# The last x tile of a stage before weight splits on VectorE, and modulation units spread over later stages

## The chip, the cores and the metric

One NeuronCore of one Trainium2 chip runs the whole program. The metric is the device time of one execution in microseconds (us); the time before is the median of three runs. TensorE is PE below (its weight loads PEld), VectorE is DVE, ScalarE ACT, GpSimd POOL, and SyncE (SP) issues most of the transfers.

## What is computed

Two blocks on x of 256 tokens by 1024. The first has a Mamba-2 mixer, a convolutional feed-forward, a differential attention and a second feed-forward; the second block, whose scale, shift and gate come from a vector c, has a sparse attention with a top-k (`dsa` in the kernel) beside a gated recurrence, and a third feed-forward. Every stage starts with an RMS norm and ends by adding to x. Cut to what the change touches:

```python
# first block, per layer:   x = x + mixer(rms_norm(x) * g);  x = x + conv_ffn(rms_norm(x) * g)
# second block:
c_act = silu(c)
mod = c_act @ w_ada + b_ada                       # w_ada is 1024 x 6144
sh1, sc1, ga1, sh2, sc2, ga2 = split(mod, 6)
xn = rms_norm(h, g_mix) * (1.0 + sc1) + sh1
q, k, v, qi, ki, wi, xr, yr, gate_a, gate_b = split(xn @ w_in + b_in)
attn = dsa_attention(q, k, v, qi, ki, wi, rel_bias)
rnn = rg_lru(causal_dwconv(xr)) * gelu(yr)
h = h + ga1 * ((sigmoid(gate_a) * (attn @ w_o_attn) + sigmoid(gate_b) * (rnn @ w_o_rnn)) @ w_out)
xn = rms_norm(h, g_ffn) * (1.0 + sc2) + sh2
val, gte = split(causal_dwconv(xn @ w_up))
h = h + ga2 * ((silu(gte) * val) @ w_down)
return rms_norm(h, g_final)
```

So `sh1` and `sc1` are needed where the sparse stage starts, `ga1` at its last product, `sh2` and `sc2` at the start of the last feed-forward and `ga2` at its last product.

## The kernel before

x lies transposed in SBUF as eight tiles of 128 features by 256 tokens. The stages run one after the other: mamba, ffn0, attn, ffn1, dsa, ffn2. Every weight product is made in fp32 from hi and lo parts: per 128 rows of a weight three matmuls of 128x128 by 256 columns, hi by hi, hi by lo and lo by hi (`mmB`, L381 to L383; in attention's token form L925 to L927). A *piece* is a weight tile of up to 128 by 1024 and serves 24 matmuls; one output tile of an up projection is one piece and one *step*.

A piece comes in a raw chunk (`load_chunk`, L230, on SP, four buffers), and is *split* (`split`, L242): ACT copies `wh` (L253), DVE subtracts for `wl` (L257; POOL does so for nine pieces). `step()` (L303) runs after each product: it calls posts that are due, splits up to two pieces ahead (as many as `LEADS` says, at most five), and issues modulation units.

**Starts of stages.** When an output tile m of a stage's last product is done, `add_x` (L508) adds it to x on DVE (L511, L513 with the gate), squares it (ACT L442, running sum on POOL L446), and `mkraw` (L395) makes hi (ACT L398) and lo (DVE L399) of the unnormalised tile, times its gain. The next stage's first four output tiles (`tileR`) use these, so that they need no norm, and are scaled afterwards. The norm itself: `rstd_bc` (L448) sums the squares with two matmuls over `sqacc` and two over the last tile's `sq` (L454), DVE (L296) and POOL (L297, a power) make the reciprocal root, PE broadcasts it (L465), ACT copies it (`rsb`, L486), then DVE makes `ny` (L495) and the lo parts `xl` (L471, or L500 with a shift). Attention needs the root per token only and has no broadcast; its first product is `tok("k", 0)` (L913), two halves of tokens with 24 matmuls each.

**Modulation.** `mod` is made by 96 *units*: one loads 256 KB of `w_ada` (L556, SP) into one of two buffers and multiplies it with silu(c) on DVE, summing along the row (L558); per two units a sum of 128 by 1 follows (`mod`, L562). `ADA_UNITS` gives for a part of a stage the steps from a to b in which n units are issued; each is ordered behind the last split on DVE (`self.pace`).

**Order.** The engines' orders are fixed when the program is built: a scheduler places the instructions by the order of the code, the dependencies and its estimate of when each can run; `after` adds a dependence that only orders.

The sparse stage's end, to which the prediction comes: eight tiles of yr (posts L1302: a gelu on ACT, `yg` on DVE L1306), then hi and lo of the eight `yg` tiles (`split_act`, L469; ACT L470, DVE L471), then per output tile m a product with `w_o_attn` and one with `w_o_rnn`, then `w_out`.

## Time and profile before

| | us |
|---|---|
| median of three runs | 1171.66 (1169.17 to 1174.88) |
| profiled execution | 1170.62 |
| its span | 1168.8, mean granted clock 0.979 |
| PE busy | 1119.3 (96%) |
| DVE busy | 949.9 (81%) |
| ACT busy | 711.2 (61%) |
| POOL busy | 171.7 (15%) |

The span runs from the first to the last instruction of the profiled execution; the rest of its time lies around it. [...] In a timeline each row has its start, its duration, engine, source line, operation, result and operands, and in brackets how long the engine had been idle before it and what ended that.

### The profile page before, as it was taken

The numbers are of one execution on the slowest core, as the hardware profiler recorded it, in microseconds if no ns is written. First come the engines' busy times: TensorE is split into PE (matmuls) and PEld (weight loads), VectorE is DVE, ScalarE is ACT, GpSimd is POOL, SyncE is SP. The second block draws the span as 40 slices with busy tenths as digits, with TensorE's granted clock in tenths as the row PEclk, the third lists the DMA queues.
The fourth block names the chain that finished last, engine by engine and source line by source line (L and its number), as shares of the span: only waits on it lengthen the run. The fifth ranks groups of instructions, "written<-read, shape, count | busy, mean of one in ns | idle before, by whom it ended". The sixth has DMA issues, their size and how long they took to land. (4 is left out here: it accounts for less than half of the span.)

```text
span 1168.8 us, 23504 instructions
## 1 busy us (share of the span) xinstructions
PE 1119.3 (96%) x9174; PEld 1090.0 (93%) x9174; DVE 949.9 (81%) x1884; ACT 711.2 (61%) x1322; POOL 171.7 (15%) x162
## 2 busy tenths in 40 slices
PE   6899998999999989999999999899999999999997
PEld 5799887999999989888899999899999999999997
DVE  5987998788899878787899988768877888888742
ACT  6567555576666546877666664465587657666541
POOL 3202665201100103222000001100100020000010
PEclk8899989999999989999999999999999999999999
DMA  8355442548766886654376667844542653554530
GB/s 307 137 181 191 161 157 79 191 170 275 262 204 238 283 288 231 199 188 153 123 248 207 213 225 257 298 175 151 180 165 94 215 214 125 203 181 176 180 132 36
DMA packets 50190, 224.80 MB, mean 192 GB/s; under 512 B 5744, under 2 KB 10496, under 8 KB 31136
## 3 DMA queue, kind: packets, MB, share of 16 engines
q1 hardware_dynamic: 41616, 211.53, 52.3%
q10 hardware_dynamic: 7056, 7.46, 2.1%
q0 software_dynamic: 1408, 4.32, 1.1%
q8 instruction: 72, 1.18, 0.4%
q14 instruction: 38, 0.31, 0.1%
HBM read 222.11 MB, written 4.25 MB: 194 GB/s over the span
## 5 line engine op out<-in xcount | busy, mean ns | idle before, releaser
L253 ACT ACTIVATE wh<-raw 128x1024 fp32r<-128x1024 f32 (+2 forms) x360 | 369.9, 1031 | 275.6 <-PE mm L382 237.9
L257 DVE TENSOR_TENSOR wl<-raw,wh 128x1024 fp32r<-128x1024 f32 (+1 forms) x351 | 419.7, 1197 | 107.4 <-ACT wh L253 105.1
L381 PE MATMUL mm<-xh,wh 128*128 128x256 f32 x1624 | 464.1, 286 | 3.0 <-DVE cv L632 1.7
L382 PE MATMUL mm<-xl,wh 128*128 128x256 f32 x1624 | 459.9, 283 | 4.1 <-DVE xl L471 3.8
L383 PE MATMUL mm<-xh,wl 128*128 128x256 f32 x1624 | 459.6, 283 | 0.1
L381 PEld LDWEIGHTS mm<-xh,wh 128*128 128x128 f32 x1624 | 307.7, 190 | 7.9 <-issue 3.5
L382 PEld LDWEIGHTS mm<-xl,wh 128*128 128x128 f32 x1624 | 307.7, 190 | 5.5 <-DVE xl L471 4.7
L383 PEld LDWEIGHTS mm<-xh,wl 128*128 128x128 f32 x1624 | 307.5, 189 | 0.6 <-DVE xc L1225 0.3
L381 PE MATMUL mm<-hh,wh 128*128 128x256 f32 x528 | 147.4, 279 | 0.0
L383 PE MATMUL mm<-hh,wl 128*128 128x256 f32 x528 | 147.4, 279 | 0.0
L382 PE MATMUL mm<-hl,wh 128*128 128x256 f32 x528 | 147.4, 279 | 0.0
L446 POOL TENSOR_TENSOR sqacc<-sqacc,sq 128x256 f32<-128x256 f32 x42 | 50.0, 1192 | 629.4 <-issue 365.2
L823 DVE SCALAR_TENSOR_TENSOR cv<-mm,par,cv 128x255 f32<-128x255 f32 x240 | 114.7, 479 | 1.8 <-ACT cv L821 0.2
L381 PEld LDWEIGHTS mm<-hh,wh 128*128 128x128 f32 x528 | 99.2, 188 | 0.0
L382 PEld LDWEIGHTS mm<-hl,wh 128*128 128x128 f32 x528 | 99.2, 188 | 0.0
L383 PEld LDWEIGHTS mm<-hh,wl 128*128 128x128 f32 x528 | 99.2, 188 | 0.0
L558 DVE SCALAR_TENSOR_TENSOR ada<-ada,silu_c 128x512 f32<-128x512 f32 x96 | 66.3, 701 | 20.8 <-DMA ada<-in_wada_dram 20.3
L821 ACT ACTIVATE cv<-mm,par 128x256 f32<-128x256 f32 x120 | 65.7, 547 | 0.3 <-PE mm L383 0.3
L381 PE MATMUL mm<-rw,wh 128*128 128x256 f32 (+2 forms) x168 | 51.8, 309 | 9.4 <-ACT wh L253 8.6
L442 ACT ACTIVATE sq<-x 128x256 f32<-128x256 f32 x49 | 20.0, 410 | 57.8 <-DVE x L511 43.7
L382 PE MATMUL mm<-rw,wh 128*128 128x256 f32 (+2 forms) x168 | 51.7, 308 | 0.0
L383 PE MATMUL mm<-rw,wl 128*128 128x256 f32 (+2 forms) x168 | 51.1, 305 | 0.0
(305 smaller groups left out, 1900.6 us busy)
## 6 DMA issues: line engine op xcount, KB each, us to landing
raw<-in_w_dram SPq DMA_DIRECT2D x148, 1024.0 KB, 4.9
ada<-in_wada_dram SPq DMA_DIRECT2D x96, 256.0 KB, 4.2
raw<-in_w_dram SPq DMA_DIRECT2D x23, 896.0 KB, 4.6
raw<-in_w_dram SPq DMA_DIRECT2D x6, 768.0 KB, 4.3
abc<-acs_scr ACTq DMA_DIRECT2D x16, 256.0 KB, 3.3
rel_bias_scr<-rel_bias_row POOLq DMA_DIRECT2D x8, 384.0 KB, 6.7
bias<-rel_bias_scr ACTq DMA_DIRECT2D x16, 128.0 KB, 2.6
x<-in_xT_dram SPq DMA_DIRECT2D x4, 256.0 KB, 4.2
```

What stands on the lines that cost most here:

```text
L253: nc.scalar.activation(wh[:, :n], src, AF.Copy)
L257: self.pace = nc.vector.tensor_tensor(wl[:, :n], src, wh[:, :n].bitcast(F32), op=ALU.subtract)
L381: nc.tensor.matmul(out, h, xh[:, k, :], start=first and a == 0, stop=False)
L382: nc.tensor.matmul(out, h, xl[:, k, :], start=False, stop=False)
L383: nc.tensor.matmul(out, l, xh[:, k, :], start=False, stop=last and a == n - 1)
L442: nc.scalar.activation(s, self.x[:, k, :], AF.Square)
L446: nc.gpsimd.tensor_tensor(self.acc, self.acc, s, op=ALU.add)
L558: i = nc.vector.scalar_tensor_tensor(t, t, 1.0, self.sc[:, h * 512:h * 512 + 512], op0=ALU.mult, op1=ALU.mult, accum_out=self.part[:, h, m ...
L821: nc.scalar.activation(c, pt, AF.Identity, scale=w(2), bias=P(cb, ct))
L823: nc.vector.scalar_tensor_tensor(c[:, d:], pt[:, :T - d], w(2 - d), c[:, d:], op0=ALU.mult, op1=ALU.add)
```

## The change

1. **`gate`.** In `mkraw`, DVE's lo part of the last x tile (k = 7) is remembered, and splits issued after it, up to the end of the next step, are ordered behind it on DVE. While the last output tile of a stage is made (`out_tile(7)`), at most `END_LEAD` = 3 pieces are split ahead, until its `add_x`.
2. **Attention's norm.** `rstd_bc` is called inside the first `tok`, and its matmuls are ordered behind the 24 of the first half of tokens.
3. **`ADA_UNITS`.** Before: nine units per up projection of ffn0 and ffn1, up to 30 in each of their down projections, 16 in attention, six in its output. Now 14 in ffn0's down projection, 16 in attention, eight and 14 in ffn1, 28 in the sparse stage (steps 4 to 57), 16 in the up projection of ffn2 (steps 12 to 39), none in the rest. `ada_until` makes up what a stage needs, should it not be there.
4. **`ada_load`.** A unit's load is issued before the DVE instruction of the unit ahead of it, in place of right before its own.
5. Buffers of the sparse stage share names (`th`, `mt1` in `xru`; `mt2` in `at2`; `kid` in a second `vT`); the modulation's buffers stay open to the end of the program.

```diff
+END_LEAD = 3
 QK_LAG, O_LAG = 3, 3
 ADA_AT = 8
-ADA_UNITS = {"up": (20, 44, 9), "down": (1, 19, 30), "attn": (5, 22, 16), "attn_out": (1, 6, 6)}
+ADA_UNITS = {"ffn0": (20, 44, 0), "ffn0_out": (1, 16, 14), "attn": (5, 22, 16), "attn_out": (0, 1, 0), "ffn1": (20, 44, 8),
+             "ffn1_out": (1, 16, 14), "dsa": (4, 58, 28), "dsa_out": (0, 1, 0), "ffn2": (12, 40, 16),
+             "ffn2_out": (0, 1, 0)}
...
             self.pace = nc.vector.tensor_tensor(wl[:, :n], src, wh[:, :n].bitcast(F32), op=ALU.subtract)
+            if self.gate is not None:
+                self.after(self.pace, self.gate)
...
-        lead = lead[self.since - 1] if self.since <= len(lead) else self.NS
+        lead = min(lead[self.since - 1] if self.since <= len(lead) else self.NS, self.cap)
         for _ in range(2):
             if self.ns < self.nu + lead:
                 self.split(self.since in POOLED.get(self.part_of, ()))
+        self.gate = None
...
-            nc.vector.scalar_tensor_tensor(l[:, k, 0:T], self.x[:, k, :], g(k), h[:, k, 0:T].bitcast(F32),
-                                           op0=ALU.mult, op1=ALU.subtract)
+            i = nc.vector.scalar_tensor_tensor(l[:, k, 0:T], self.x[:, k, :], g(k), h[:, k, 0:T].bitcast(F32),
+                                               op0=ALU.mult, op1=ALU.subtract)
+            if k == 7 and self.now:
+                self.gate = i
...
-    def rstd_bc(self, parts, n, bcast=True):
+    def rstd_bc(self, parts, n, bcast=True, behind=None):
 
         nc = self.nc
         st = self.ax()
         for i, p in enumerate(parts):
             for tt in range(2):
-                nc.tensor.matmul(st[:, tt:tt + 1], p[:, tt * 128:tt * 128 + 128], self.ones,
+                mm = nc.tensor.matmul(st[:, tt:tt + 1], p[:, tt * 128:tt * 128 + 128], self.ones,
                                  start=(i == 0 and tt == 0), stop=i == len(parts) - 1, skip_group_check=True)
+                if behind is not None:
+                    self.after(mm, behind)
...
+        if m == 7:
+            self.cap = self.NS
+
+    def out_tile(self, m):
+
+        if m == 7:
+            self.cap = END_LEAD
...
+    def ada_load(self):
+        m, h = self.adal[self.adan]
+        self.adan += 1
+        t = self.adap.tile([128, D // 2], F32, name="ada")
+        w = self.a["wada"]
+        self.nc.sync.dma_start(t, bass.AP(tensor=w.tensor, offset=w.offset + (2 * m + h) * 65536,
+                                          ap=[[D // 2, 128], [1, D // 2]]))
+        self.adat.append(t)
...
+            while len(self.adat) < 2 and self.adan < len(self.adal):
+                self.ada_load()
             m, h = self.adaq.popleft()
-            t = self.adap.tile([128, D // 2], F32, name="ada")
-            nc.sync.dma_start(t, bass.AP(tensor=w.tensor, offset=w.offset + (2 * m + h) * 65536,
-                                         ap=[[D // 2, 128], [1, D // 2]]))
+            t = self.adat.popleft()
...
+    def ada_until(self, m):
+
+        n = 2 * m - (96 - len(self.adaq))
+        if n > 0:
+            self.due = 0.0
+            self.ada(n)
...
-        self.rstd_bc([self.acc, self.sq7], D, bcast=False)
-        rs = self.rs
         xop = {"k": (rkv[:, 0], rkv[:, 1]), "v": (rkv[:, 0], rkv[:, 1]), "q": rq}
         v = tl("v", [128, 2, 1024])
         tT = {}
+        norm = []
...
-                    nc.tensor.matmul(o, xl[:, k, s], wh[:, cs], start=False, stop=k == 7)
+                    mm = nc.tensor.matmul(o, xl[:, k, s], wh[:, cs], start=False, stop=k == 7)
+                if not norm:
+                    self.rstd_bc([self.acc, self.sq7], D, bcast=False, behind=mm)
+                    norm.append(self.rs)
...
+                    self.ada_until(16 if n == "dsa" else 40)
```

Where the instructions stand now. The first place is the start of attention on DVE, at the add of the last x tile (`x`, L511 before and L522 now; `rw` and `xl0` are lo parts of raw tiles, `ada` modulation units, `wl` splits). Before:

```order
L558 SCALAR_TENSOR_TENSOR ada_5031,mod_parts_3206<-ada_5031,silu_c_3207 128x512 [waits DMAHW3_49]
L558 SCALAR_TENSOR_TENSOR ada_5034,mod_parts_3206<-ada_5034,silu_c_3207 128x512 [waits DMAHW4_49]
L257 TENSOR_TENSOR wl_5328<-raw_5104,wh_5327 128x1024 [waits PE_49,Activation_49]
L562 SCALAR_TENSOR_TENSOR mod_3205<-mod_parts_3206,par_81 128x1 [waits DVE_49]
L511 TENSOR_TENSOR x_83<-mm_5272,x_83 128x256 [waits PE_49]
L897 TENSOR_TENSOR lam2_5367<-par_81 128x128
L257 TENSOR_TENSOR wl_5357<-raw_5104,wh_5356 128x1024 [waits Activation_49]
L399 SCALAR_TENSOR_TENSOR rw_4536<-x_83,par_81,rw_4536 128x256 [waits DVE_49,Activation_49]
L399 SCALAR_TENSOR_TENSOR xl0_4538<-x_83,par_81,xh0_4537 128x256 [waits Activation_49]
```

and with the change:

```order
L406 SCALAR_TENSOR_TENSOR rw_4505<-x_83,par_81,rw_4505 128x256 [waits DVE_49,Activation_49]
L406 SCALAR_TENSOR_TENSOR xl0_4507<-x_83,par_81,xh0_4506 128x256 [waits Activation_49]
L522 TENSOR_TENSOR x_83<-mm_5187,x_83 128x256 [waits PE_49]
L935 TENSOR_TENSOR lam2_5276<-par_81 128x128
L943 TENSOR_SCALAR sg_5283<-par_81 128x1
L937 TENSOR_REDUCE lam_5278<-lam2_5276 128x2 [waits DVE_49]
L406 SCALAR_TENSOR_TENSOR rw_4505<-x_83,par_81,rw_4505 128x256 [waits Activation_49]
L406 SCALAR_TENSOR_TENSOR xl0_4507<-x_83,par_81,xh0_4506 128x256 [waits Activation_49]
L261 TENSOR_TENSOR wl_5262<-raw_4968,wh_5261 128x1024
L261 TENSOR_TENSOR wl_5268<-raw_5036,wh_5267 128x1024 [waits DMAHW2_49]
```

Before, two units, a split and a `mod` sum stand ahead of the last add, and a split behind it ahead of its lo parts. With the change the add comes right behind the lo part of the tile before it, and the splits come behind its lo parts.

On PE at the same place, the sum over the last tile's squares (`sq`) stood inside the first token tile before:

```order
L926 MATMUL mm_5387<-wl_5269,rw_4536 128x256 [waits DVE_49]
L927 MATMUL mm_5387<-wh_5268,rw_4536 128x256
L925 MATMUL mm_5387<-wh_5268,rw_4536 128x256
L454 MATMUL ax_5376<-onec_86,sq_5350 128x1 [waits Activation_49]
L454 MATMUL ax_5376<-onec_86,sq_5350 128x1
L926 MATMUL mm_5387<-wl_5269,rw_4536 128x256
L927 MATMUL mm_5387<-wh_5268,rw_4536 128x256
```

and now stands, with the sum over `sqacc`, behind its last matmul (`rw` with `wh_5183` is the end of the first half; `wh_5151` begins the second):

```order
L962 MATMUL mm_5288<-wh_5183,rw_4505 128x256 [waits Activation_49]
L963 MATMUL mm_5288<-wl_5184,rw_4505 128x256
L964 MATMUL mm_5288<-wh_5183,rw_4505 128x256 [waits DVE_49]
L463 MATMUL ax_5313<-onec_86,sqacc_4591 128x1 [waits Pool_49]
L463 MATMUL ax_5313<-onec_86,sqacc_4591 128x1
L463 MATMUL ax_5313<-onec_86,sq_5255 128x1 x2
L962 MATMUL mm_5288<-wh_5151,rw_4505 128x256
L963 MATMUL mm_5288<-wl_5152,rw_4505 128x256
```

The second place is the start of the sparse stage on DVE (`gmdsa` is the gain with modulation, `rs` the root's first step). Before:

```order
L257 TENSOR_TENSOR wl_9464<-raw_9254,wh_9463 128x1024 [waits PE_49,Activation_49]
L511 TENSOR_TENSOR x_83<-mm_9408,x_83 128x256 [waits PE_49]
L257 TENSOR_TENSOR wl_9491<-raw_9254,wh_9490 128x1024 [waits Activation_49]
L399 SCALAR_TENSOR_TENSOR rw_8693<-x_83,gmdsa_8694,rw_8693 128x256 [waits DVE_49,Activation_49]
L558 SCALAR_TENSOR_TENSOR ada_9221,mod_parts_3206<-ada_9221,silu_c_3207 128x512 [waits DMAHW5_49]
L558 SCALAR_TENSOR_TENSOR ada_9256,mod_parts_3206<-ada_9256,silu_c_3207 128x512 [waits DMAHW6_49]
L562 SCALAR_TENSOR_TENSOR mod_3205<-mod_parts_3206,par_81 128x1 [waits DVE_49]
L296 TENSOR_SCALAR rs_9508<-ax_9503 128x2 [waits PE_49]
```

and with the change, where no unit is left and the last add comes behind a lo part:

```order
L522 TENSOR_TENSOR x_83<-mm_9169,x_83 128x256 [waits PE_49]
L261 TENSOR_TENSOR wl_9253<-raw_9043,wh_9252 128x1024 [waits DMAHW7_49,Activation_49]
L406 SCALAR_TENSOR_TENSOR rw_8587<-x_83,gmdsa_8588,rw_8587 128x256 [waits DVE_49,Activation_49]
L522 TENSOR_TENSOR x_83<-mm_9256,x_83 128x256 [waits PE_49]
L1290 TENSOR_SCALAR bgb_9787<-par_81 128x8
L302 TENSOR_SCALAR rs_9349<-ax_9344 128x2 [waits PE_49]
L406 SCALAR_TENSOR_TENSOR rw_8587<-x_83,gmdsa_8588,rw_8587 128x256 [waits DVE_49,Activation_49]
L261 TENSOR_TENSOR wl_9329<-raw_9043,wh_9328 128x1024
L261 TENSOR_TENSOR wl_9335<-raw_9109,wh_9334 128x1024 [waits DMAHW2_49]
```

The third place is the end of the loop of yr on DVE, with the eight lo parts (`xl0<-yg`) that `w_o_rnn`'s product reads. Before:

```order
L257 TENSOR_TENSOR wl_11392<-raw_10871,wh_11391 128x512 [waits PE_49,Activation_49]
L1306 TENSOR_TENSOR yg_9926<-xc_9922,th_11425 128x256 [waits Activation_49]
L257 TENSOR_TENSOR wl_11429<-raw_10999,wh_11428 128x1024 [waits DMAHW0_49,PE_49,Activation_49]
L1306 TENSOR_TENSOR yg_9926<-xc_9922,th_11460 128x256 [waits DVE_49,Activation_49]
L257 TENSOR_TENSOR wl_11464<-raw_10999,wh_11463 128x512 [waits PE_49,Activation_49]
L1306 TENSOR_TENSOR yg_9926<-xc_9922,th_11472 128x256 [waits Activation_49]
L471 TENSOR_TENSOR xl0_11476<-yg_9926,xh0_11475 128x256 [waits Activation_49] x5
L471 TENSOR_TENSOR xl0_11476<-yg_9926,xh0_11475 128x256 [waits DVE_49,Activation_49]
```

and with the change, in which units (`ada`) and their sums stand between (two more units and a sum lie a few rows above):

```order
L1313 SCALAR_TENSOR_TENSOR xc_9782<-rr_9783,ii_9784 128x256 [waits DVE_49]
L1312 TENSOR_TENSOR ii_9784<-ii_9784,yg_9786 128x256
L1313 SCALAR_TENSOR_TENSOR xc_9782<-rr_9783,ii_9784 128x256 [waits DVE_49]
L261 TENSOR_TENSOR wl_11342<-raw_10898,wh_11341 128x1024 [waits DMAHW5_49,PE_49,Activation_49]
L586 SCALAR_TENSOR_TENSOR ada_11270,mod_parts_3206<-ada_11270,silu_c_3207 128x512 [waits DMAHW3_49]
L1349 TENSOR_TENSOR yg_9786<-xc_9782,xru_11377 128x256 [waits Activation_49]
L590 SCALAR_TENSOR_TENSOR mod_3205<-mod_parts_3206,par_81 128x1 [waits DVE_49]
L261 TENSOR_TENSOR wl_11381<-raw_10898,wh_11380 128x512 [waits PE_49,Activation_49]
L1349 TENSOR_TENSOR yg_9786<-xc_9782,xru_11389 128x256 [waits Activation_49]
L482 TENSOR_TENSOR xl0_11393<-yg_9786,xh0_11392 128x256 [waits Activation_49] x8
```

## Rows read from the trace of the kernel before

**Rows 1.** The page, part 1: busy time and its share of the span, by engine.

```profile
PE 1119.3 (96%) x9174; PEld 1090.0 (93%) x9174; DVE 949.9 (81%) x1884; ACT 711.2 (61%) x1322; POOL 171.7 (15%) x162
```

**Rows 2.** The waits of PE: engine, line, releaser: us in total, times, longest us.

```profile
PE ax L454 <- ACT sq L442: 6.5, 2, 3.5
PE ax L465 <- POOL rs L297: 6.3, 5, 3.5
...
PE ax L454 <- POOL sqacc L446: 2.5, 3, 1.0
```

**Rows 3.** Windows of 10 us at three starts: busy times, then PEclk, DMA share, GB/s.

```profile
430.00:440.00 10.00, 9.04 (x54) 9.04 (x55) 5.56 (x17) 4.29 (x9) 0.71 (x1) 0.66 0.80 268
...
550.00:560.00 10.00, 8.72 (x67) 8.00 (x66) 10.00 (x17) 5.19 (x11) 3.40 (x4) 0.98 0.84 279
560.00:570.00 10.00, 10.00 (x75) 10.00 (x75) 6.04 (x16) 5.73 (x12) 0.71 (x1) 0.85 0.33 116
...
750.00:760.00 10.00, 7.05 (x38) 6.84 (x37) 7.58 (x17) 2.23 (x4) 0.71 (x1) 0.71 0.76 269
760.00:770.00 10.00, 10.00 (x81) 10.00 (x81) 8.52 (x22) 8.05 (x18) 1.19 (x2) 0.95 0.19 43
```

**Rows 4.** Timeline at the start of attention, DVE and then PE.

```profile
427.38 0.69 DVE L558 SCALAR_TENSOR_TENSOR ada<-ada,silu_c 128x512 f32<-128x512 f32 x1 [1.46 <-DMA ada<-in_wada_dram]
...
428.71 1.22 DVE L257 TENSOR_TENSOR wl<-raw,wh 128x1024 fp32r<-128x1024 f32 x1
...
429.98 0.42 DVE L511 TENSOR_TENSOR x<-mm,x 128x256 f32<-128x256 f32 x1
...
430.96 0.59 PE L454 MATMUL ax<-onec,sq 128*128 128x1 f32 x2 [3.51 <-ACT sq L442]
```

**Rows 5.** Timeline at the start of ffn1, DVE and then PE.

```profile
558.71 0.41 DVE L511 TENSOR_TENSOR x<-mm,x 128x256 f32<-128x256 f32 x1
...
557.75 0.38 PE L381 MATMUL mm<-rw,wh 128*128 128x256 f32 x1 [0.73 <-ACT rw L398]
558.56 0.61 PE L454 MATMUL ax<-onec,sqacc 128*128 128x1 f32 x4 [0.42 <-POOL sqacc L446]
```

**Rows 6.** Timeline at the start of the sparse stage, DVE and then PE.

```profile
745.56 0.69 DVE L558 SCALAR_TENSOR_TENSOR ada<-ada,silu_c 128x512 f32<-128x512 f32 x1 [2.84 <-DMA ada<-in_wada_dram]
...
746.18 0.42 DVE L511 TENSOR_TENSOR x<-mm,x 128x256 f32<-128x256 f32 x1
746.51 0.21 DVE L562 SCALAR_TENSOR_TENSOR mod<-mod_parts,par 128x1 f32<-128x1 f32 x1
746.64 0.68 DVE L558 SCALAR_TENSOR_TENSOR ada<-ada,silu_c 128x512 f32<-128x512 f32 x1
...
753.22 0.42 DVE L511 TENSOR_TENSOR x<-mm,x 128x256 f32<-128x256 f32 x1
...
754.20 0.57 PE L454 MATMUL ax<-onec,sq 128*128 128x1 f32 x2 [2.95 <-ACT sq L442]
```

**Rows 7.** The page, part 5: groups: busy us, mean ns; idle before, releaser.

```profile
L257 DVE TENSOR_TENSOR wl<-raw,wh 128x1024 fp32r<-128x1024 f32 (+1 forms) x351 | 419.7, 1197 | 107.4 <-ACT wh L253 105.1
...
L558 DVE SCALAR_TENSOR_TENSOR ada<-ada,silu_c 128x512 f32<-128x512 f32 x96 | 66.3, 701 | 20.8 <-DMA ada<-in_wada_dram 20.3
```

**Rows 8.** Windows of 10 us behind the top-k, columns as in Rows 3, DVE third.

```profile
840.00:850.00 10.00, 10.00 (x80) 9.79 (x79) 5.92 (x11) 6.84 (x13) 0.54 (x1) 1.00 0.65 225
850.00:860.00 10.00, 10.00 (x87) 9.37 (x85) 7.54 (x21) 9.62 (x27) 0.00 (x0) 1.00 0.37 126
```

**Rows 9.** Timeline at the end of the loop of yr, DVE and then PE.

```profile
904.45 1.22 DVE L257 TENSOR_TENSOR wl<-raw,wh 128x1024 fp32r<-128x1024 f32 x1 [0.55 <-ACT wh L253]
...
906.87 0.69 DVE L257 TENSOR_TENSOR wl<-raw,wh 128x512 fp32r<-128x512 f32 x1 [0.86 <-ACT wh L253]
...
907.81 2.43 DVE L471 TENSOR_TENSOR xl<-yg,xh 128x256 fp32r<-128x256 f32 x7
...
908.29 0.39 PE L382 MATMUL mm<-xl,wh 128*128 128x256 f32 x1
```

**Rows 10.** A window of 80 us in ffn2's up projection, columns as in Rows 3.

```profile
1000.00:1080.00 80.00, 80.00 (x677) 80.00 (x676) 68.32 (x112) 51.04 (x84) 0.00 (x0) 1.00 0.52 186
```

## What the change does to the time: a prediction

> **What bounds the kernel now.** I read the busy times first [rows 1]: PE has 1119.3 of 1168.8 us, VectorE 949.9. PE is the bound, but what it does not lose to matmuls is what a change of order can win, and that has two parts: waits, and matmuls at a low clock. The list of PE's waits [rows 2] gives the first part. Beside the first weight piece at the very start, which nothing here touches, the largest entries belong to the normalisation at the start of a stage: 6.5 us for the squares of the last x tile (twice), 6.3 us for the reciprocal root from POOL (five times, 1.3 us on average), and 2.5 us for the running sum of squares. [...]
>
> Then the timelines of the three starts [rows 4 to 6] tell why PE waits. At the start of attention PE goes on at 430.96, after 3.51 us of waiting, with the sum over the last x tile's squares. That tile's add ran on VectorE at 429.98, and VectorE was not waiting for PE in between: from 427.38 it had modulation and a weight split in front of the add, and the unit at 427.38 had itself been 1.46 us late, for its load. At ffn1 the last add is at 558.71, behind the operands of the tile before; PE waits 0.73 and 0.42 us. At the sparse stage a unit that waited 2.84 us for its load heads the queue at 745.56, and the last add is at 753.22; PE waits 1.0 us, the longest of its waits for the running sum [rows 2], and then, up to 754.20, 2.95 us. So the last x tile is late because VectorE takes weight splits and modulation first, and PE's clock falls behind each of the three waits.
>
> **The change, part by part.** The sum is made against the profiled execution: 1170.62 us (span 1168.8 and 1.8 around it), 1.04 below the median of the three runs, 1171.66.
>
> *Attention's start.* Removed: the wait of 3.51 us [rows 4], and the low clock behind it. The window 430 to 440 loses (1 - 0.66) x 10 = 3.4 us to the clock [rows 3]; some 0.5 of it lies inside the wait, so 2.9 are matmuls. Together 6.4 us. In the new order no unit or split stands between the last two adds and only small work follows; the matmuls of the norm come behind all 24 matmuls of the first token tile, which need the last x tile only for their last three. PE makes 677 matmuls in 80 us where nothing holds it [rows 10], 24 in 2.8 us; it reaches these three 2.4 us after it began, and the add, the hi parts on ACT and the two lo parts on VectorE take under 2. What remains lies between nothing and the 1.0 us that PE waits at the sparse stage for the running sum; I take 0.3, near the lower end, since the sums now have a whole tile as cover. Gain 6.1, with 4.5 (that wait and some clock behind it) and 6.4 as ends.
>
> *ffn1's start.* The units of the attention output move away (none is left in that loop), so eight adds come earlier. Removed: 0.73 + 0.42 us [rows 5] and a clock loss of 0.2 + 1.5 us in the windows from 550 and 560 [rows 3]; 2.85 together. The broadcast of the root still needs its trip over VectorE and POOL, and PE may meet it: 0 to the 1.3 us of the average [rows 2], I take 0.45. Gain 2.4, ends 1.0 (that wait and some clock) and 2.85.
>
> *The sparse stage's start.* Removed: 1.0 + 2.95 us [rows 2, 6] and 2.9 + 0.5 us of clock [rows 3], 7.4 together. Here the sum over the last tile now stands behind only ten matmuls of the first tile and the broadcast five behind it, so the root's trip is not wholly covered; with only three pieces split ahead the next pieces are close as well. I take 1.4 (the average of 1.3 for this wait and a little), with 0 and 3.5 (its longest case) as ends. Gain 6.0, ends 3.9 and 7.4.
>
> *ffn0's and ffn2's starts.* Norm matmuls move by two to eleven places; the same wait may shrink or grow by its average of 1.3 us. I take -0.2.
>
> *The moved units.* A unit costs VectorE 0.70 us [rows 7], the small sum per two units 0.13 more (from 746.51 to 746.64 [rows 6]). Before, the last of the 96 ran at the sparse stage's start; now 28 run inside it, 28 x 0.70 + 14 x 0.13 = 21.4 us, and 16 in ffn2, 12.2 us. A late load is what could hurt most there: at 745.56 a unit held up VectorE for 2.84 us, and the add of an x tile, which needs nothing from it, stands directly behind [rows 6]. [...] No row of before shows the sparse stage with units in it, so I price places. Around the top-k, eight units (6.1 us) are met by VectorE idle time of 4.1 + 2.5 us in the windows from 840 and 850 [rows 8]: nothing to 2 us, I take 0.3. In the loop of yr four units and two sums come in, 3.1 us, and there VectorE has only 0.55 + 0.86 us of idle [rows 9] before the eight lo parts that start at 907.81; PE reads the first of them at 908.29, as soon as it is written. So these parts get late by 3.1 - 1.4, about 1.7, and a little less as units can overlap their neighbours: I take 1.4, ends 0 and 3.5 (all 3.1 and some clock). Elsewhere in the stage a piece is split several pieces ahead, each of them 24 matmuls or 2.8 us, and a unit of 0.7 us hides behind that lead. In ffn2 VectorE is busy for 68.32 of 80 us [rows 10]; 16 units in 28 steps of 2.8 us add 12.2 in 78 us, 0.157, and 0.854 + 0.157 makes 1.01 of PE's time. An excess of 0.01 over 78 us is 0.8 us, which the lead hides: 0, with a loss of 2 as the other end. POOL gets nothing. SP issues the same 96 loads, each before the unit ahead of its own, so that the 20.3 us that VectorE sat idle for loads [rows 7] mostly go, where they mattered inside the starts already counted.
>
> Sum: 6.1 + 2.4 + 6.0 - 0.2 - 0.3 - 1.4 = 12.6 off: 1158.0 for an execution like the profiled one, **1159.0** for the median.
>
> **The rivals.**
> *1. The sparse stage takes back more.* The lo parts of the recurrent output come late by all of 3.1 us (1.7 more than taken), PE's clock falls behind that wait as it did at ffn1 after 1.15 us of waiting (1.7), and the top-k's end passes on 1.7 more. 5.1 back: 1164. For it: PE takes the first of these operands as soon as it is written [rows 9]. Against it: a unit can overlap the end of its neighbour, and yr's steps may catch up.
> *2. Loads still come late.* A unit that waits for its load blocks what stands behind it on VectorE. Before, 96 units cost 20.3 us of such idle time, 0.21 each; if loading ahead changes nothing, 28 units bring 5.9 us into a stage with tighter operands. Half of it reaching PE gives 1162, all of it 1165. For it: the block at 745.56 [rows 6]. [...] Against it: a load now has the whole distance between two units.
> *3. The clock stays low at the starts anyway*, since a shorter wait for the root or for a piece takes the place of the old one (the lead of three pieces helps that). Then only waits are won: 3.2 + 0.7 + 2.6, less 1.9 as before, 4.6 off: 1167. For it: at ffn1 two waits under 1 us were enough [rows 5].
> *4. Slower: VectorE becomes the bound of the sparse stage and of ffn2.* That happens from the point at which the units exceed both the idle time and the lead of split pieces. If only the idle time counted (6.6 around the top-k, 1.4 at yr), 21.4 - 8.0 = 13.4 us in the sparse stage and 0.8 in ffn2 would reach PE: 14.2, as much as the three starts gain (14.5), and with two or three low clocks of 1.7 behind such waits 3 to 5 us slower: 1175. Against it: pieces are split several steps ahead, and VectorE is idle 6.6 us around the top-k while PE is not [rows 8].
>
> **How the numbers follow.** My forecast has 0.60, rival 1 0.20, rival 2 0.07, rival 3 0.08, rival 4 0.05. The range goes from 1153, where all three starts give their upper ends (16.65) the losses of 0.3 and 1.4 fall away and the other two starts give 1.3, to 1167, which takes in rivals 1 and 2 and part of rival 3; below and above it some 0.15 remain. A measurement of this kernel tells about 0.5% (5.9 us) from no change: faster means under 1165.8. The forecast lies there nearly always, rivals 1 and 2 mostly, rival 3 a third of the time: faster 0.82. Rival 3's rest and parts of 1 and 2: same 0.13. Slower 0.05.
>
> **What would show it.** In the changed profile PE's waits for ACT's squares should be gone or under 1 us, the windows at the starts of attention and ffn1 should show a clock of 1.00, that of the sparse stage 0.9 or more. A wait of 1 to 2 us for the lo parts should stand in the recurrent output's first products. VectorE should have almost no idle time in the middle of ffn2, with PE at full busy share. The prediction is wrong if the clock at the starts stays low, if PE waits for weight splits in the sparse stage, or if units there still wait long for their loads.

## The result, and the profile of the changed kernel

The changed kernel takes 1157.09 us (median of four runs, 1156.02 to 1157.68) against 1172.03 of the kernel before (median of four): the ratio is 0.9898, with a 95% interval of 0.9871 to 0.9924. The forecast was 1159.0 in a range from 1153 to 1167. The span of the profiled execution went from 1168.8 to 1155.9 us.

The page of the changed kernel, part 1, answers to [rows 1]: PE is busy 8 us less and still 96% of its span, VectorE has the same work.

```profile
PE 1111.2 (96%) x9174; PEld 1084.1 (94%) x9174; DVE 946.9 (82%) x1884; ACT 712.6 (62%) x1322; POOL 178.3 (15%) x162
```

The waits of PE in the changed kernel (engine, line, releaser: us in total, times, longest), against [rows 2]. The waits for ACT's squares are gone, that for the running sum has come down from 2.5 to 1.2 us (what is left lies at the program's start), and those for the root have grown from 6.3 to 9.2 us:

```profile
PE ax L476 <- POOL rs L303: 9.2, 7, 3.5
...
PE mm L389 <- DVE xl L482: 4.8, 3, 2.2
...
PE ax L463 <- POOL sqacc L455: 1.2, 1, 1.2
```

Windows of 10 us of the changed kernel at the starts of attention, ffn1, the sparse stage and ffn2 (columns as in [rows 3]; PEclk is the share of its full clock that PE was granted: in the kernel before it is 0.50 from 430.0 to 436.5 us, where 128x256 matmuls start 0.21 us apart, and 1.00 from 437.0 to 440.0, where they start 0.12 apart). The clock is 1.00 at the first three, where it had been 0.66, 0.85 and 0.71. At ffn2 it is 0.83: one low interval stands there as one did before (0.83 in the window from 980), now right behind the wait of 1.25 us for the root:

```profile
430.00:440.00 10.00, 10.00 (x86) 10.00 (x86) 7.13 (x11) 5.71 (x9) 4.39 (x3) 1.00 0.90 320
550.00:560.00 10.00, 8.62 (x71) 8.22 (x70) 7.18 (x16) 5.75 (x12) 1.73 (x1) 1.00 0.35 120
740.00:750.00 10.00, 9.36 (x79) 9.15 (x78) 8.87 (x18) 6.07 (x14) 1.12 (x2) 1.00 0.75 234
950.00:960.00 10.00, 8.75 (x61) 8.54 (x60) 4.83 (x9) 4.46 (x12) 1.75 (x1) 0.83 0.32 105
```

The timeline of the changed kernel, first VectorE at attention's start and VectorE at the end of yr's loop, then PE there (answers to [rows 4, 9]). The last add now waits for PE's product and for nothing else; VectorE had been idle for 4.17 us. At yr a unit and a `mod` sum (the sum that follows two units) run shortly ahead of the lo parts, and PE waits 1.13 us for the first of them:

```profile
426.40 0.42 DVE L522 TENSOR_TENSOR x<-mm,x 128x256 f32<-128x256 f32 x1 [4.17 <-PE mm L390]
...
890.86 0.69 DVE L586 SCALAR_TENSOR_TENSOR ada<-ada,silu_c 128x512 f32<-128x512 f32 x1
...
891.80 0.22 DVE L590 SCALAR_TENSOR_TENSOR mod<-mod_parts,par 128x1 f32<-128x1 f32 x1
...
892.88 1.42 DVE L482 TENSOR_TENSOR xl<-yg,xh 128x256 fp32r<-128x256 f32 x4
...
893.34 0.39 PE L389 MATMUL mm<-xl,wh 128*128 128x256 f32 x1 [1.13 <-DVE xl L482]
```

Where the time went can be read by laying the two timelines over each other, matmul by matmul, and taking the step of the distance between the same matmuls in each stretch (us, minus is earlier):

| stretch | forecast, with its ends | measured |
|---|---|---|
| attention's start | -6.1 (-6.4 to -4.5) | -6.4 |
| attention's inside and output | not priced | -1.0 |
| ffn1's start | -2.4 (-2.85 to -1.0) | -3.2 |
| the sparse stage's start | -6.0 (-7.4 to -3.9) | -6.85 |
| around the top-k | +0.3 (0 to +2) | 0.0 |
| yr and the lo parts | +1.4 (0 to +3.5) | +1.5 |
| starts of ffn0 and ffn2 | +0.2 (-1.3 to +1.3) | +0.4 and +1.15 |
| ffn2's products | 0 (0 to +2) | +0.6 |
| program's start and mamba, untouched | not priced | +0.8 |
| sum | -12.6 | -13.0 |

The last line but one is mostly chance: in mamba PE's clock was low for 6.8 us in this execution where it had been low for 3.4 in the one before (0.66 and 0.83 in the window from 180), behind the same wait of 2.69 us in both.

The result is that of the forecast, but the forecast holds several causes that the change brings together. The experiments take them apart.

### The profile page after: what moved, and what is told of

Same layout as the page of the kernel before. It is cut to its first block, busy times and chain, and to the rows that moved or that the text cites. A ratio compares the mean times of both kernels' runs of the same rounds, so it can differ in the third digit from the quotient of the medians.

```text
span 1155.9 us, 23508 instructions
## 1 busy us (share of the span) xinstructions
PE 1111.2 (96%) x9174; PEld 1084.1 (94%) x9174; DVE 946.9 (82%) x1884; ACT 712.6 (62%) x1322; POOL 178.3 (15%) x162
## 5 line engine op out<-in xcount | busy, mean ns | idle before, releaser
L388 PE MATMUL mm<-rw,wh 128*128 128x256 f32 (+2 forms) x168 | 50.7, 302 | 8.4 <-ACT wh L257 8.4
L389 PE MATMUL mm<-rw,wh 128*128 128x256 f32 (+2 forms) x168 | 50.2, 299 | 0.1
L388 PEld LDWEIGHTS mm<-rw,wh 128*128 128x128 f32 (+1 forms) x168 | 33.2, 198 | 8.7 <-ACT wh L257 8.4
```

Source lines behind the costliest of these rows:

```text
L388: nc.tensor.matmul(out, h, xh[:, k, :], start=first and a == 0, stop=False)
L389: nc.tensor.matmul(out, h, xl[:, k, :], start=False, stop=False)
```

## The experiments

Four theories stood against each other: units and splits together delay the last x tile (A, that of the prediction), the splits alone (B), the place of the norm's sum alone (C), the units alone (D), and of D again the time they take (D1) or their late loads (D2).

### One part of the change alone, or one left out

**The first part alone**, on the kernel before (units in their old places, no load ahead, the norm where it was):

```diff
+            if self.gate is not None:
+                self.after(self.pace, self.gate)
...
+        if m == 7:
+            self.cap = END_LEAD
```

> The kernel before with the first part alone: later splits behind the last lo part, three pieces ahead at a stage's end. Theory A (units and splits together stand ahead of the last x tile's add, and each start needs both gone): at the starts of attention and of the sparse stage two units still stand right ahead of the last add, each may wait for its load, so PE keeps waits of 1 to 3 us there and the low clock behind them; ffn1's start loses its wait. Time 1166 to 1170. Theory B (the splits were the delay, the units hardly matter): all three starts recover, 1158 or less, since the sparse stage gets no units.

Measured: 1172.32 us, ratio 1.0042 (1.0023 to 1.0061), slightly slower than before. PE's wait for the squares is 5.4 us in two times, nearly that of [rows 2], and the wait for the root has grown to 8.9:

```profile
PE ax L476 <- POOL rs L303: 8.9, 7, 3.5
...
PE ax L463 <- ACT sq L451: 5.4, 2, 3.4
```

The timeline of this kernel on VectorE at attention's start: no split is left before the last add, but two units are, the first of them 2.32 us late for its load:

```profile
428.08 0.69 DVE L585 SCALAR_TENSOR_TENSOR ada<-ada,silu_c 128x512 f32<-128x512 f32 x1 [2.32 <-DMA ada<-in_wada_dram]
...
428.73 0.69 DVE L585 SCALAR_TENSOR_TENSOR ada<-ada,silu_c 128x512 f32<-128x512 f32 x1
...
429.60 0.42 DVE L522 TENSOR_TENSOR x<-mm,x 128x256 f32<-128x256 f32 x1
```

B falls. A was too hopeful here too: ffn1's start kept its waits of 0.74 and 0.43 us.

**The second part alone**, on the kernel before:

```diff
+                if not norm:
+                    self.rstd_bc([self.acc, self.sq7], D, bcast=False, behind=mm)
```

> The kernel before with the second part alone: attention's norm behind its first 24 matmuls. Theory A: the last x tile is as late as before, so the wait of 3.5 us moves from the sum of squares to the first tile's last three matmuls, which need that tile's hi and lo parts, and may be longer by the time these take; 1170 to 1173. Theory C (the wait was only one for the sum, placed too early): the wait and the low clock at attention go, 1165 to 1166.

Measured: 1170.35 us, ratio 1.0019 (0.9997 to 1.0042). The wait did move, as A had it. PE in this kernel at attention's start, at the first tile's last three matmuls:

```profile
433.21 0.38 PE L959 MATMUL mm<-wh,rw 128*128 128x256 f32 x1 [4.00 <-ACT rw L403]
```

C falls: 4.00 us for the tile's hi part in place of 3.51 for its square.

**The third and fourth parts alone**: the changed kernel without the gate, the lead of three and the moved norm.

```diff
-            if self.gate is not None:
-                self.after(self.pace, self.gate)
...
-END_LEAD = 3
+END_LEAD = 5
...
+        self.rstd_bc([self.acc, self.sq7], D, bcast=False)
-                if not norm:
-                    self.rstd_bc([self.acc, self.sq7], D, bcast=False, behind=mm)
```

> The changed kernel without its first two parts: units spread and loaded ahead, but splits may go ahead of the last x tile and attention's norm stands where it stood. Theory A: two splits (2.4 us) still stand ahead of the last add at attention and at the sparse stage, so PE keeps waits of about 1 to 2 us and in part the low clock; at yr the same wait of 1.1 us as in the changed kernel. 1160 to 1166. Theory D (only the units and their loads delayed the tiles): as fast as the changed kernel, 1156 to 1158. Theory B: hardly faster than before, 1168 to 1172.

Measured: 1152.67 us, ratio 0.9877 (0.9830 to 0.9925): all of the gain and more (every one of its four executions, 1151.44 to 1154.34, lies under every one of the changed kernel's). None of the theories had it below the changed kernel. The timeline of this kernel at the sparse stage's start, VectorE and then PE. Splits do stand around the last add (one just ahead, one between it and its lo part), and PE waits for nothing: the split ahead had itself waited 1.56 us for ACT, so VectorE had room, and the sum over the squares stands 11 matmuls into the first tile:

```profile
735.52 1.23 DVE L261 TENSOR_TENSOR wl<-raw,wh 128x1024 fp32r<-128x1024 f32 x1 [1.56 <-ACT wh L257]
736.66 0.41 DVE L520 TENSOR_TENSOR x<-mm,x 128x256 f32<-128x256 f32 x1
...
737.63 1.22 DVE L261 TENSOR_TENSOR wl<-raw,wh 128x1024 fp32r<-128x1024 f32 x1 [0.48 <-ACT wh L257]
738.77 0.48 DVE L404 SCALAR_TENSOR_TENSOR rw<-x,gmdsa,rw 128x256 fp32r<-128x256 f32 x1
...
738.17 0.50 PE L461 MATMUL ax<-onec,sq 128*128 128x1 f32 x4
```

The windows of this kernel at the starts of attention and of ffn2 show a clock of 1.00 (against 0.83 at ffn2 with the whole change):

```profile
430.00:440.00 10.00, 10.00 (x86) 10.00 (x85) 4.89 (x6) 6.69 (x10) 3.38 (x2) 1.00 0.63 226
...
950.00:960.00 10.00, 9.55 (x79) 9.34 (x79) 8.25 (x18) 7.27 (x16) 0.71 (x1) 1.00 0.34 111
```

A falls in one half: the units, with the waits for their loads, were the delay; the splits were not.

**The units back in their old places**, all else as in the change (what is left of the 96 comes at the end of ffn1):

```diff
-ADA_UNITS = {"ffn0": (20, 44, 0), "ffn0_out": (1, 16, 14), "attn": (5, 22, 16), "attn_out": (0, 1, 0), "ffn1": (20, 44, 8),
-             "ffn1_out": (1, 16, 14), "dsa": (4, 58, 28), "dsa_out": (0, 1, 0), "ffn2": (12, 40, 16),
+ADA_UNITS = {"ffn0": (20, 44, 9), "ffn0_out": (1, 19, 30), "attn": (5, 22, 16), "attn_out": (1, 6, 6), "ffn1": (20, 44, 9),
+             "ffn1_out": (1, 19, 30), "dsa": (4, 58, 0), "dsa_out": (0, 1, 0), "ffn2": (12, 40, 0),
...
+            if mods:
+                self.ada(len(self.adaq))
```

> The changed kernel with the units where they were before (9, 30, 16, 6, 9 and the rest by the end of ffn1), but each loaded one ahead. Theory A: attention's start gains most of its 6.4 us, ffn1's some; at the sparse stage units still stand ahead of the last add, and about half of its 6.9 us stays; in return the wait of 1.1 us for the lo parts behind yr is absent and the time there falls by 1.5. 1160 to 1165. Theory B: faster than the changed kernel, 1154 to 1156, since nothing is given back in the sparse stage.

Measured: 1176.26 us, ratio 1.0057 (1.0031 to 1.0083): slower than before, and far from both expectations. At attention PE waits 2.27 us for the last tile's hi part and 1.20 for its lo part, in front of which a unit now stands, since the gate took the splits away from there and left it to the units:

```profile
432.83 0.69 DVE L586 SCALAR_TENSOR_TENSOR ada<-ada,silu_c 128x512 f32<-128x512 f32 x1 [0.99 <-DMA ada<-in_wada_dram]
...
433.44 0.48 DVE L406 SCALAR_TENSOR_TENSOR rw<-x,par,rw 128x256 fp32r<-128x256 f32 x1
...
432.28 0.39 PE L962 MATMUL mm<-wh,rw 128*128 128x256 f32 x1 [2.27 <-ACT rw L405]
...
433.98 0.39 PE L964 MATMUL mm<-wh,rw 128*128 128x256 f32 x1 [1.20 <-DVE rw L406]
```

These two waits replace the one of 3.51 us of before, and laid over the kernel before this place is 0.4 us better. What makes the kernel slower than before lies right behind, 4.4 us: the root of attention's norm, now behind the first tile, stands on VectorE behind a unit that waits 1.74 us for its load, and PE then waits 2.77 us for the normalised k from POOL (`uk`), with 1.7 us of low clock behind it:

```profile
437.94 0.69 DVE L586 SCALAR_TENSOR_TENSOR ada<-ada,silu_c 128x512 f32<-128x512 f32 x1 [1.74 <-DMA ada<-in_wada_dram]
...
450.93 0.66 PE L995 MATMUL ax<-con,uk 128*128 128x128 f32 x4 [2.77 <-POOL uk L991]
```

So the first two parts do not bring the gain where units are left at the starts.

### Time of the units, or their loads

**Units spread, but loaded right before their use**, without gate and moved norm:

```diff
-            while len(self.adat) < 2 and self.adan < len(self.adal):
-                self.ada_load()
+            self.ada_load()
```

> Units spread as in the change, but each loaded right before its use as before; no gate, no moved norm. Theory D1 (what counted was the time that units take ahead of the last adds): same as the run with units alone, within 1 us, since no unit is left at the starts; single units in the sparse stage wait for their load, in stretches with room. Theory D2 (late loads were the delay): VectorE sits idle for loads by 0.2 us per unit as before, some of it in tight stretches, and the kernel is 3 to 6 us slower than the run with units alone.

Measured: 1152.82 us, ratio 0.9860 (0.9831 to 0.9889), beside 1152.67 with loads ahead (on another chip). On the chip of this run the changed kernel took 1158.85. **Loads ahead alone**, on the kernel before:

> The kernel before with the fourth part alone: units in their old places, each loaded one ahead. Theory D1 (what counts is the time that units and the order around them take ahead of the last adds): the waits of 3.5, 1.0 and 2.95 us at the starts shrink by at most the 1.5 to 2.8 us that a unit was late there; time within 0.3% of the kernel before. Theory D2 (late loads were the delay): the waits and the low clock at attention and at the sparse stage go, 1158 or less.

Measured: 1169.43 us, ratio 0.9999 (0.9981 to 1.0017). The waits of VectorE and of PE in this kernel: units waited 26.0 us for their loads in place of the 20.3 of [rows 7], PE's waits for the squares stand at 5.5, and those for the running sum have grown from 2.5 to 5.9:

```profile
DVE ada L584 <- DMA ada<-in_wada_dram: 26.0, 21, 4.2
```

```profile
PE ax L461 <- POOL sqacc L453: 5.9, 4, 2.1
PE ax L461 <- ACT sq L449: 5.5, 2, 3.2
```

So the load ahead is worth nothing that can be measured in either place. At ffn1 D1 holds: no unit of attention's output waits for its load, here or in the kernel before, and the waits of 0.7 and 0.4 us stand at that start as long as these units do. At attention and at the sparse stage the run does not decide between D1 and D2, since one unit ahead was not early enough: late units still stood there, by 2.68 and 4.22 us where it had been 1.46 and 2.84 [rows 4, 6]. VectorE in this kernel:

```profile
426.12 0.69 DVE L584 SCALAR_TENSOR_TENSOR ada<-ada,silu_c 128x512 f32<-128x512 f32 x1 [2.68 <-DMA ada<-in_wada_dram]
...
749.99 0.69 DVE L584 SCALAR_TENSOR_TENSOR ada<-ada,silu_c 128x512 f32<-128x512 f32 x1 [4.22 <-DMA ada<-in_wada_dram]
```

No run had units at these two starts with all their loads there in time, so what part of the delay is the units' own time and what part their loads stays open. And with the units spread none of them waits for a load in the sparse stage or in ffn2, loaded ahead or not (11.4 us of such waits without, 8.6 with, all in the down projections of ffn0 and ffn1), so D2's price for late loads in the sparse stage was never paid. What the runs show is that units must not stand before a stage's last adds as they were loaded here.

### What the first two parts cost

In the changed kernel POOL's power for the root takes 1.73 us at ffn1 and a split starts on VectorE 0.06 us before it. The timeline of the changed kernel at ffn1's start, VectorE, POOL and PE:

```profile
552.63 0.16 DVE L302 TENSOR_SCALAR rs<-ax 128x2 f32<-128x2 f32 x1 [0.25 <-PE ax L463]
552.81 1.23 DVE L261 TENSOR_TENSOR wl<-raw,wh 128x1024 fp32r<-128x1024 f32 x1
...
552.87 1.73 POOL L303 TENSOR_TENSOR rs<-rs,half 128x2 f32<-128x2 f32 x1 [3.67 <-DVE rs L302]
...
554.65 0.60 PE L476 MATMUL ax<-con,rs 128*128 128x128 f32 x3 [1.24 <-POOL rs L303]
```

In the kernel before the same power took 0.71 us, with VectorE free:

```profile
561.89 0.71 POOL L297 TENSOR_TENSOR rs<-rs,half 128x2 f32<-128x2 f32 x1 [3.39 <-DVE rs L296]
```

It is the gate that puts the held splits there. To test it the splits behind a norm wait for a small copy of the root on VectorE, which waits for POOL, and the lead of three lasts until that norm. Beside it ran the changed kernel again, and the units alone without any in yr's eight steps (four go to ffn0's down projection in their place).

```diff
             bc = self.rstd_bc([self.acc, self.sq7], D)
+            self.cap = self.NS
+            if self.now:
+                d = self.tp.tile([128, 2], F32, name="rs")
+                self.gate = nc.vector.tensor_copy(d, self.rs)
...
-        if m == 7:
+        if m == 7 and len(self.raws) != 1:
             self.cap = self.NS
```

> The changed kernel once more, beside the three below on one chip. 0.987 to 0.992 of the kernel before; waits of 0.7, 1.2, 0.6 and 1.2 us for POOL's root at the starts of ffn0, ffn1, the sparse stage and ffn2.

> The changed kernel with the splits that follow a norm held, by a small copy of the root on VectorE, until POOL's power has ended. Theory P (the power takes 1.6 to 1.75 us in place of 0.7 because a split starts on VectorE just ahead of it, which is what the gate brought about): the power takes 0.7 to 0.9 us at all four starts, PE's waits for it fall to 0.5 us or less at ffn0, ffn1 and ffn2, and with the low clock behind ffn2's wait gone the kernel is 2 to 4 us faster than the changed kernel. Theory Q (the waits for the root come from the place of the broadcast on PE alone): the power keeps its length and the waits stay; time within 1 us of the changed kernel, or slower by up to 2 if the held splits come late.

Measured: the changed kernel 1158.85 us, ratio 0.9907 (0.9878 to 0.9936); with the held splits 1153.46, ratio 0.9867 (0.9838 to 0.9896), 5.4 us less on the same chip. Its timeline at ffn1's start, VectorE, POOL and PE again:

```profile
552.10 0.16 DVE L302 TENSOR_SCALAR rs<-ax 128x2 f32<-128x2 f32 x1 [1.38 <-PE ax L463]
553.08 0.17 DVE L499 COPY rs<-rs 128x2 f32<-128x2 f32 x1 [0.82 <-POOL rs L303]
553.16 1.22 DVE L261 TENSOR_TENSOR wl<-raw,wh 128x1024 fp32r<-128x1024 f32 x1
...
552.34 0.71 POOL L303 TENSOR_TENSOR rs<-rs,half 128x2 f32<-128x2 f32 x1 [3.67 <-DVE rs L302]
...
553.10 0.78 PE L476 MATMUL ax<-con,rs 128*128 128x128 f32 x3 [0.46 <-POOL rs L303]
```

P holds at ffn0, ffn1 and ffn2 (0.70 to 0.71 us in place of 1.61 to 1.74, PE's waits 0.45 to 0.46 in place of 0.73 to 1.25); at the sparse stage, where it is the last lo part (0.48 us) that runs beside the power and not a split, it kept its 0.90. How much of the 5.4 us the shorter power itself brings is not shown: the two profiled executions, whose spans are 1154.0 and 1152.8 us, lie only 1.2 apart, and the second has a low interval of the clock behind ffn1's root that the first has not. Nor did a run have the moved norm with the units spread and no gate; alone it changed nothing (1.0019). The same thing was tried once more where the change does nothing, at the program's first norm, on top of the kernel of the next section:

```diff
-POOLED = {"mamba": (1, 3, 5, *range(22, 44, 4))}
+POOLED = {"mamba": (3, 5, *range(22, 44, 4))}
...
-            for _ in range(self.NS - 3):
-                self.split()
...
+            if not self.now:
+                d = self.tp.tile([128, 2], F32, name="rs")
+                self.gate = nc.vector.tensor_copy(d, self.rs)
```

> The run without units in yr, with one thing more, at the very first norm, which the change does not touch: two splits that stood ahead of it are made behind it, held until POOL's power has ended. Theory P: that power takes 0.7 us in place of 1.63 and PE's wait of 1.4 us for the root at 17.8 shrinks to 0.5; the later splits may cost up to 1 us behind it. 0 to 1 us faster than the run without units in yr. Theory Q: the power keeps 1.63 us.

The power in this kernel takes 0.71 us in place of 1.63, as P has it, and PE's wait for this root is gone. The time is 1151.63 us, ratio 0.9846 (0.9821 to 0.9871), not to be told from the kernel without it. PE now waits a little later, 0.54 us for a result of VectorE and 0.89 for a hi part, where the kernel without it does not wait; which of the later waits take the gain back is not taken apart.

```profile
16.27 0.71 POOL L304 TENSOR_TENSOR rs<-rs,half 128x2 f32<-128x2 f32 x1 [1.38 <-DVE rs L303]
...
31.79 0.36 PE L389 MATMUL mm<-xh,wh 128*128 128x256 f32 x1 [0.54 <-DVE ru L422]
...
34.33 0.39 PE L389 MATMUL mm<-xh,wh 128*128 128x256 f32 x1 [0.89 <-ACT xh L480]
```

### Units in the sparse stage

The third and fourth parts alone, with no unit in yr's eight steps:

```diff
+        self.hold = True
         for t in range(8):
             self.tileB(W, 8, xh, xl, yr_post(t), delay=2)
+        self.hold = False
...
-ADA_UNITS = {"ffn0": (20, 44, 0), "ffn0_out": (1, 16, 14), "attn": (5, 22, 16), "attn_out": (0, 1, 0), "ffn1": (20, 44, 8),
+ADA_UNITS = {"ffn0": (20, 44, 0), "ffn0_out": (1, 16, 18), "attn": (5, 22, 16), "attn_out": (0, 1, 0), "ffn1": (20, 44, 8),
```

> The kernel with units spread and loaded ahead, without the gate and without the moved norm, and in addition with no unit in the eight steps of yr; four more units run in ffn0's down projection. Theory Y (the units in yr make the eight lo parts late): PE's wait of 1.1 us for them goes, and the matmuls behind come 1.4 to 1.6 us earlier than in the run with units alone, about 1151; ffn0's down projection shows no new wait. Theory Z (the wait comes from the splits there or from ACT): it stays at 1 us.

Measured: 1151.91 us, ratio 0.9850 (0.9821 to 0.9880), and on another chip 1152.13, ratio 0.9849 (0.9824 to 0.9874):

> The run without units in yr once more, beside the one above on one chip: 1150 to 1153.

The wait of 1.1 us is gone in both. Laid over the run with units alone, the products behind yr come 1.25 us earlier than those before it; in the second of the two a low interval of the clock after another wait (0.5 us, for a transfer) had taken 1.7 at 775, and the first has none there. The lo parts in the second, with no unit ahead of them:

```profile
889.08 0.69 DVE L262 TENSOR_TENSOR wl<-raw,wh 128x512 fp32r<-128x512 f32 x1 [0.86 <-ACT wh L258]
889.68 0.42 DVE L1349 TENSOR_TENSOR yg<-xc,xru 128x256 f32<-128x256 f32 x1
890.02 1.09 DVE L481 TENSOR_TENSOR xl<-yg,xh 128x256 fp32r<-128x256 f32 x3
```

Y holds for the wait. In the time it hardly shows: 0.9 us below the units without loads ahead on the same chip, with executions that overlap. Last, how near VectorE is to its limit in the sparse stage, again on the third and fourth parts alone:

```diff
-ADA_UNITS = {"ffn0": (20, 44, 0), "ffn0_out": (1, 16, 14), "attn": (5, 22, 16), "attn_out": (0, 1, 0), "ffn1": (20, 44, 8),
-             "ffn1_out": (1, 16, 14), "dsa": (4, 58, 28), "dsa_out": (0, 1, 0), "ffn2": (12, 40, 16),
+ADA_UNITS = {"ffn0": (20, 44, 0), "ffn0_out": (1, 16, 14), "attn": (5, 22, 0), "attn_out": (0, 1, 0), "ffn1": (20, 44, 8),
+             "ffn1_out": (1, 16, 14), "dsa": (4, 58, 44), "dsa_out": (0, 1, 0), "ffn2": (12, 40, 16),
```

> As the run with units alone, but the 16 units of attention run in the sparse stage too, which then has 44 in place of 28. Theory V (VectorE has room for units everywhere in the sparse stage but in the steps of yr): the two units more in yr and their sum, 1.5 us, make PE's wait for the lo parts 2.3 to 2.8 us in place of 1.1, a low clock of 1.7 us may follow, and nothing else there gets slower: 1154 to 1157. Theory W (VectorE becomes the bound of the sparse stage): 16 units of 0.70 us come out late, 5 to 11 us slower than with 28, with waits for splits and for the attention's operands there: 1158 to 1164.

Measured: 1162.09 us, ratio 0.9934 (0.9912 to 0.9957), 9.4 slower than with 28 (on another chip). It is not a clean test: with attention's units gone ffn1's down projection got 24 units in place of 14, and two came to stand ahead of the last add again, with the old wait behind them:

```profile
736.30 0.69 DVE L584 SCALAR_TENSOR_TENSOR ada<-ada,silu_c 128x512 f32<-128x512 f32 x1 [1.45 <-DMA ada<-in_wada_dram]
...
738.85 0.42 DVE L520 TENSOR_TENSOR x<-mm,x 128x256 f32<-128x256 f32 x1
...
739.83 0.38 PE L461 MATMUL ax<-onec,sq 128*128 128x1 f32 x2 [2.84 <-ACT sq L449]
```

Of its distance to the run with 28, 5.0 us come in at that start, and 9.5 within the stage, in small waits for a transfer, for gate operands, for a hi and for lo parts, with one low interval; attention, now without units, gives 3.2 back. W is nearer than V.

## Why the prediction was right, and where it was not

**The starts** were the gain, as forecast: 6.4, 3.2 and 6.85 us against 6.1, 2.4 and 6.0, and the low clock there went with the waits. The reading behind it was half right. "VectorE takes weight splits and modulation first" holds for modulation alone: without it the splits may stand where they stood, and PE waits for none of them. I had seen one split between the units and the add, and counted it as part of the delay; without the units it lies in time that VectorE has. The sum could not notice, since it priced the change as a whole; that it comes within 0.4 us of the measured one is luck in part, as the terms that it lacked or put at nothing (-1.0, +0.6 and +0.8) nearly cancel.

**ffn1** gained 0.35 more than its upper end: small stalls of later products in that start went too, which no term held, although its root cost 1.24; and the sum misses 1.0, most of it in attention's output, which the units left.

**ffn0's and ffn2's starts** were priced as a loss of 0.2, by the average of 1.3 us of the waits for the root. That average was misread: 3.5 of the 6.3 us lie inside mamba and 1.4 at the program's start, and the root's waits at ffn0 and ffn2 were 0.46 and 0.45. The two starts cost 0.4 and 1.15, and ffn1's root cost 1.24 where I took 0.45. The step that failed is the one by which splits that move behind the last lo part cost nothing: they land beside POOL's power and make it 0.9 to 1.0 us longer. Each start alone lies within the 1.3 allowed, both together (1.55) do not.

**The sparse stage** came out as forecast: nothing around the top-k, 1.5 at yr (1.4 forecast), ffn2's products without a wait for splits. Rival 1 did not happen: the wait of 1.13 us had no low clock behind it (1.00 in the windows of 10 us from 890 and 900). Rival 2 did not happen: units' loads came late for 8.8 us in all in the changed kernel, all of it in the down projections of ffn0 and ffn1 and none in the sparse stage. Rival 3 did not happen: the clock is 1.00 at the three starts. Neither did rival 4 with 28 units; with 44 the stage loses 9.5 us. One sign came only in part: VectorE was to have almost no idle time in the middle of ffn2 (1.01 of PE's time by the sum), and it was busy for 75.76 of 80 us, with PE at full busy share:

```profile
990.00:1070.00 80.00, 80.00 (x677) 80.00 (x676) 75.76 (x150) 50.91 (x83) 0.00 (x0) 1.00 0.68 235
```

**Loads ahead** were said to save idle time "where they mattered inside the starts already counted". They saved nothing: alone they leave the time as it was, and left out they cost nothing.

The version that is best here is the third and fourth parts without the first two and without units in yr: 1151.91 and 1152.13 us, some 5 us below the changed kernel; the third and fourth parts with units in yr (1152.67) cannot be told from it. Attention without units looked 3 us faster in the run with 44; units in ffn0's down projection in their place weren't tried.

## What to carry to other kernels

Work that nobody waits for, and that can itself come late, belongs neither ahead of the last tile of a stage nor ahead of an operand that is read as it is written; everywhere else it hid here, up to a point (with 28 units the sparse stage lost 1.5 us, at yr; with 44 it lost 9.5 more). When one engine's order is changed to clear a path, look at what takes the cleared place beside the path's next step on another engine (here a split beside POOL's power, 1.73 us in place of 0.71 at ffn1). And run each part of such a change alone: the first two of the four, together, gave back about a third of what the third one won.

## What was not expected of the hardware

POOL's power over 128x2 numbers takes 0.70 to 0.72 us when VectorE is free around its start or has only instructions over 128x1 there, and 1.61 to 1.82 when a split of a 128x1024 tile (two operands in SBUF) starts between 0.17 us before it and 0.03 after. A split that starts 0.16 us or more behind the power leaves it at 0.70 or 0.71. Shorter VectorE instructions with two operands in SBUF lengthen it by less: a last lo part of 0.48 us begun 0.16 or 0.17 us ahead makes it 0.89 to 0.91, and a unit of 0.69 us begun 0.02 behind it makes it 1.28 (the sparse stage, units back in their old places). Wherever it was longer than 0.72 us, the power ends 0.55 to 0.59 us after the VectorE instruction beside it has ended. That held for the root's power at all six norms of every one of the fourteen profiled kernels, among them the same norm with and without the split in front. No run has a long VectorE instruction with a single operand in SBUF at that place, and why the power gets longer is not shown. The price here is about 1 us for a power beside a split.
